# Layer norm statistics of the first three output tiles moved to ScalarE, and the selector matrices in a transfer of their own

## The chip, the core and the metric

One core of one Trainium2 chip runs the whole program. The metric is the time of one execution in device microseconds (us). The kernel before was timed three times: 891.20, 893.87 and 894.52 us, with the median at 893.87 us. One further execution was profiled. It took 891.03 us, and the profile covers 889.1 us of it (the span).

## What is computed

One inference step of a one-layer decoder, for 512 prompt tokens and 32 sample tokens, all in fp32. The front scales and shifts the input by vectors that come from a condition `c` (nine rows: one for the prompt, eight for the samples). Then follow one large input projection, a windowed attention (branch A) and a gated delta rule (branch B). The back merges the branches, multiplies by `w_out` and applies a layer norm to each token's row of 1024 numbers.

```python
def layer_front(x, c, w_cond, b_cond, w_in):
    shift, scale, gate = jnp.split(jax.nn.silu(c) @ w_cond + b_cond, 3, axis=-1)
    h = x * (1 + scale[:, None]) + shift[:, None]
    return gate, split_columns(h @ w_in)
...
    merged = jax.nn.sigmoid(ga) * (ya @ w_branch_a) + jax.nn.sigmoid(gb) * (yb @ w_branch_b)
    r = (ALPHA * x + gate[:, None] * (merged @ w_out)).astype(jnp.float32)
    mu = jnp.mean(r, axis=-1, keepdims=True)
    var = jnp.mean(jnp.square(r - mu), axis=-1, keepdims=True)
    return ((r - mu) * lax.rsqrt(var + LN_EPS)).astype(dtype) * ln_g + ln_b
```

## The kernel before

**Recording and scheduling.** The kernel does not issue instructions as it is read. `body` records every operation with its operands; `Recorder.schedule` (line 450 on) then sets one fixed order for each engine by a list scheduler with its own cost table, and `emit` issues them. All engines run their own list in order. For that reason nearly all instructions carry line 727. A change of one cost or one dependency anywhere can move instructions in other places too, as the scheduler breaks its ties anew.

**Split products.** Each large product is done as three passes of TensorE on a high and a low part of both factors (`hhi`, `hlo` are the input, `hi`, `lo` a tile of weights, `pp` the PSUM bank). A projection tile has 128 output features by 544 tokens, in two halves of 272 tokens; a half is 24 matmuls. The pool of `pp` has two banks, so a half can start once the half before the previous one has been copied out of its bank.

**The front** (lines 902 to 1030). SyncE (its queue is SPq in the profile) issues all loads in one queue: `cT`, the condition weights `wc` in 16 pieces of 512 KB, the bias `bT`, the constants `cst`, the transposed input `xT` and the first weights `W`. `cst` is one table of 330 columns: the identity `ident`, the selector matrices `selc` and `selg`, `low16` and `dmask`. `cond_block` multiplies `wc` by the condition, copies the rows to `Y`, and multiplies `Y` by `selc` to turn the scale of each feature into a column (`pg<-cst,Y`). `gate_rows` uses `selc` and `selg` together, 73 columns, much later.

**The back** (lines 2292 to 2399). `product_out` multiplies the merged rows by `w_out`, for n = 0 and 1 (512 output columns each) and tt = 0 to 3 (128 tokens each); tile 3 is done in pieces of 256 columns. The sum over one piece leaves PSUM in `scalar_tensor_tensor` into `r` (times the gate `gp`), then `tensor_add` adds the scaled input `xr`, then `bn_stats` takes the piece's statistics. All three run on VectorE (DVE). `norm_out` (line 2332) joins the statistics with `bn_aggr` into `mv`, ScalarE (ACT) takes the square root, and VectorE does the subtraction with the weight `lng` (1024 columns), a reciprocal, and two halves with `lnb`. Each half is then stored to `y_p`. `samples_out` does the same for the 32 sample rows between n = 0 and n = 1. Tile 3 of n = 1 has a rank that puts it ahead on VectorE.

**A place in the middle.** Near the end of the attention for the prompt, four ACT table switches, a reciprocal of 512 columns (`kq`), the copies out of `pp` into `spare` (an activation on ScalarE, then a product on VectorE that frees the bank), the copy `crow` and the product `vr` stand close together. The change does not edit that code, but the new order differs there.

Of the kernel before, what the change touches and what calls it, by code (L numbers as in the profile page):

```python
# [11 lines left out]
F32 = mybir.dt.float32  # L12
F32R = mybir.dt.float32r
AF = mybir.ActivationFunctionType
# [5 lines left out]
D = 1024  # L20
# [58 lines left out]
def shape_constants():  # L79

    p = np.arange(128)
    b4, i4, h8 = p // 32, p // 8 % 4, p % 8
    blk = {}
    blk["ident"] = np.eye(128)
    blk["selc"] = (p[:, None] % 32 == np.arange(9)[None, :])
    tok = np.arange(2 * NS)
    blk["selg"] = (p[:, None] % 32 == 1 + tok[None, :] % NS // 4)
    blk["triu"] = (p[:, None] <= p[None, :])
    same = p[:, None] // 4 == p[None, :] // 4
    blk["btri"] = same & (p[:, None] <= p[None, :])  # L90
    blk["bones"] = same
    blk["low16"] = np.where(p[:, None] % 32 >= 16, -1.0, 0.0)
    blk["strict4"] = same & (p[:, None] < p[None, :])
    blk["dmask"] = np.where(p[:, None] <= p[None, :], 0.0, -BIG)
    blk["dmask_s"] = np.where(same & (p[:, None] <= p[None, :]), 0.0, -BIG)
    blk["bmask"] = (p[:, None] % 32 // 4 == np.arange(8)[None, :])
    blk["quarter"] = np.where(p[:, None] % 32 == p[None, :] % 32, 0.25, 0.0)
    blk["hmask"] = (p[:, None] % 4 == np.arange(4)[None, :])
    sab = np.zeros((128, 4, 4))
    for h4 in range(4):  # L100
        for g in range(2):
            sab[4 * g + h4::16, h4, g] = 1.0
# [677 lines left out]
def body(ctx, tc, io):  # L780
    rec = Recorder()
    pe, ve, se, ge, sp = rec.engines()
    mv = sp
# [28 lines left out]
        return psp.tile([128, 512], F32, name="pp", tag="pp")  # L812


    cst = consts.tile([128, CONST[0].shape[1]], F32, name="cst")
    tables = {"early": cst}

    def take(gen, n):
        for _ in range(n):
# [3 lines left out]
    def C(name, where="early"):  # L823
        a, n = CCOLS[name]
        return tables[where][:, a:a + n]
# [38 lines left out]
    def to_features(pv, k, rows):  # L864

        for i in range(4):
            pe.matmul(pv[:, k + i, 0:9], rows[:, 128 * i:128 * i + 128], C("selc"), start=True, stop=True)

    f16 = lambda t: t[:, :128].rearrange("p (a b) -> p a b", b=16)

# [15 lines left out]
    n = CONST[1].shape[1]  # L886
# [8 lines left out]
    with ExitStack() as fctx:  # L895
# [35 lines left out]
        def cond_block(part, at, m, other):  # L931
# [18 lines left out]
            pv = ps[:, 256:256 + 16 * m].rearrange("p (a b) -> p a b", b=16)  # L950
            with rec.together():
                for i in range(m):
                    pe.matmul(pv[:, i, 0:9], Y[:, 128 * i:128 * i + 128], C("selc"), start=True, stop=True)
# [55 lines left out]
        with rec.together():  # L1009
            for t in range(4):  # L1010
                m = 128 if t < 3 else 16
                pe.matmul(pv[0:m, 16 * t:16 * t + 9], Y[:, 128 * t:128 * t + m], C("selc"), start=True, stop=True)
# [713 lines left out]

    def sample_decays(nd):

        tables["d"] = d0.tile([128, CONST[2].shape[1]], F32, name="cd")
# [393 lines left out]

    def gate_rows():

        sel = cst[:, CCOLS["selc"][0]:CCOLS["selc"][0] + 73]
        yield gates_over
        for n in range(2):
            w = slice(512 * n, 512 * n + 512)
# [184 lines left out]
    bn = [o1.tile([128, 4 if tt == 3 else 2, 6], F32, name=f"bn{tt}") for tt in range(5)]  # L2314
    parts = lambda k: ((mhi[k], 0), (mhi[k], 1), (mlo[k], 0))

    def product_out(tt, c0, c1):
# [26 lines left out]
    def samples_out():  # L2344
# [14 lines left out]
        ve.bn_stats(bn[4][:, 0, :], q)  # L2359
        mv = o2.tile([128, 4], F32, name="mv")  # L2360
        ve.bn_aggr(mv[:, 0:2], bn[4][:, 0, :])
# [13 lines left out]
    for n in range(2):  # L2375
        if n:
            samples_out()
        for tt in range(4):
            xr, q = load_x(tt, n), r[tt]
            step = 256 if tt == 3 else 512  # L2380
            for c in range(512 * n, 512 * n + 512, step):
                po = product_out(tt, c, c + step)
                w = slice(c, c + step)
                at_end = tt == 3 and c == 768
                rec.rank = -2 * (n and tt == 3)
                with rec.together() if at_end else nullcontext():
                    ve.scalar_tensor_tensor(q[:, w], po, 0.5, gp[:, w], op0=OP.mult, op1=OP.mult)
                    ve.tensor_add(q[:, w], q[:, w], xr[:, c - 512 * n:c - 512 * n + step])
                    ve.bn_stats(bn[tt][:, c // step, :], q[:, w])
                    if at_end:  # L2390
                        mv = o2.tile([128, 4], F32, name="mv")
                        ve.bn_aggr(mv[:, 0:2], bn[tt].rearrange("p a b -> p (a b)"))
                rec.rank = 0
            if n:
                rec.rank = -2 * (tt == 3)
# [35 lines left out]
def lay_out(x):  # L2431
# [7 lines left out]
    d = {  # L2439
        "bias_p": bias_p,  # L2440
        "bias_s": bias_s,
        "const": CONST[0],
        "const_g": CONST[1],
        "const_d": CONST[2],
        "const_s": CONST[3],
        "const_q": CONST[4],
        "x": rows,
        "xT": rows.T.reshape(KT, 128, NT).transpose(1, 0, 2),
        "cT": c.T.reshape(KT, 128, 9).transpose(1, 0, 2),
# [59 lines left out]
```

## Time and profile before

| | us |
|---|---|
| median of three runs | 893.87 |
| profiled execution | 891.03 |
| its span | 889.1 |
| TensorE (PE) busy | 868.8 (98%) |
| VectorE (DVE) busy | 646.1 (73%) |
| ScalarE (ACT) busy | 453.9 (51%) |

The four times, 891.03, 891.20, 893.87 and 894.52 us, fall into two pairs. The profile's times are counted from the start of the span. A row of the timeline has the start, the duration, the engine, the instruction with its output and inputs, and in brackets the idle time just before it with what ended it. A row of the waits has the total, the number and the longest wait. A row of the windows has the length of the stretch, the busy time with the number of instructions for PE, PEld, DVE, ACT and POOL, the granted clock, the busy share of the DMA engines and the GB/s moved. A row of the groups has the count, the total and the mean ns of one. The clock granted to TensorE was 0.996 over the run.

### The profile page before, as it was taken

How to read it: one execution, taken by the hardware profiler on the slowest of the kernel's cores; microseconds unless marked ns; L12 is line 12 of the kernel's file. 1: busy time of each engine (PE TensorE's matmuls, PEld its weight loads, DVE VectorE, ACT ScalarE, POOL GpSimd, SP SyncE). 2: the span in 40 equal slices, each digit the busy share in tenths (PEclk: the TensorE clock that was granted, in tenths of full speed). 3: DMA queues.
4: the chain of work that ended last, by engine and by line, in shares of the span. 5: the costliest groups of instructions: out<-in, count | busy, mean ns of one | idle time of the engine just before them, and what ended most of it. 6: DMA issues, size and time to landing. Idle time of an engine off the chain costs nothing.

```text
span 889.1 us, 20805 instructions
## 1 busy us (share of the span) xinstructions
PE 868.8 (98%) x8212; PEld 821.2 (92%) x8212; DVE 646.1 (73%) x1338; ACT 453.9 (51%) x1083; POOL 70.0 (8%) x173
## 2 busy tenths in 40 slices
PE   8999999999999999999999998999999999999995
PEld 7899999899999999999999897999999999999884
DVE  3675447653379997489988647556999699998558
ACT  3555378844478834579734566653442222334321
POOL 0120011100001200000200100011010000001000
PEclk9999999999999999999999999999999999999998
DMA  9965785776879788888888675659969899987963
GB/s 343 337 207 178 228 281 180 237 265 197 273 218 316 242 278 297 279 274 272 272 272 263 223 231 166 199 186 281 349 228 375 275 421 403 352 306 236 355 211 120
DMA packets 106910, 236.18 MB, mean 266 GB/s; under 512 B 30407, under 2 KB 62481, under 8 KB 104125
## 3 DMA queue, kind: packets, MB, share of 16 engines
q1 hardware_dynamic: 106812, 234.86, 77.7%
q8 instruction: 64, 1.05, 0.5%
q14 instruction: 34, 0.27, 0.1%
HBM read 218.53 MB, written 103.97 MB: 363 GB/s over the span
## 4 chain that ended last, share of the span: by engine, by line
PE 89%; ACT 3%; DMA 2%; DVE 2%; SPq 1%; issue 1%; DVEq 0%; ACTq 0%
PE pp L727 68%; PE pg L727 9%; PE pd L727 8%; PE pb L727 4%; DMA wc<-in_w_cb 2%; SPq L727 1%; ACT L727 1%; DVE r L727 1%; DMA S<-in_state_delta 1%; ACT sq L727 1%; ACT hi L727 0%; DVE lo L727 0%; DVE zt L727 0%; ACT ext L727 0%; ACT acc L727 0%
## 5 line engine op out<-in xcount | busy, mean ns | idle before, releaser
L727 PE MATMUL pp<-hhi,hi 128*128 128x272 f32 x1360 | 399.8, 294 | 2.5 <-DVE spare L727 1.5
L727 PE MATMUL pp<-hlo,hi 128*128 128x272 f32 x1360 | 400.2, 294 | 0.0
L727 PE MATMUL pp<-hhi,lo 128*128 128x272 f32 x1360 | 399.2, 294 | 0.0
L727 PEld LDWEIGHTS pp<-hhi,hi 128*128 128x128 f32 x1360 | 256.3, 188 | 5.8 <-issue 1.8
L727 PEld LDWEIGHTS pp<-hhi,lo 128*128 128x128 f32 x1360 | 256.1, 188 | 3.9 <-issue 2.7
L727 PEld LDWEIGHTS pp<-hlo,hi 128*128 128x128 f32 x1360 | 256.6, 189 | 2.5 <-issue 1.5
L727 ACT ACTIVATE hi<-wt 128x1024 fp32r<-128x1024 f32 (+1 forms) x101 | 103.7, 1026 | 162.0 <-PE pp L727 137.3
L727 DVE TENSOR_TENSOR lo<-wt,hi 128x1024 fp32r<-128x1024 f32 (+1 forms) x101 | 119.0, 1179 | 80.3 <-ACT hi L727 78.6
L727 DVE SCALAR_TENSOR_TENSOR acc<-ext,cw,acc 128x568 f32<-128x568 f32 x72 | 57.8, 803 | 1.1 <-ACT acc L727 0.4
L727 ACT ACT_TABLE_LOAD x36 | 46.2, 1283 | 2.5 <-DVE acc L727 0.9
L727 DVE TENSOR_TENSOR slab<-slab 128x512 f32<-128x512 f32 (+1 forms) x66 | 43.1, 670 | 4.5 <-DMA slab<-in_ks 3.2
L727 DVE TENSOR_REDUCE slab<-slab 128x8 f32<-128x512 f32 (+2 forms) x66 | 42.9, 662 | 2.9 <-ACT slab L727 2.6
L727 ACT ACTIVATE zt<-pp 128x272 f32<-128x272 f32 x48 | 18.7, 390 | 41.0 <-PE pp L727 39.5
L727 PE MATMUL pp<-ybl,hi 128*128 128x272 f32 x128 | 37.0, 289 | 0.0
L727 PE MATMUL pp<-ybh,lo 128*128 128x272 f32 x128 | 37.0, 289 | 0.0
L727 PE MATMUL pp<-ybh,hi 128*128 128x272 f32 x128 | 36.8, 288 | 0.0
L727 ACT ACTIVATE P<-P,st 128x256 f32<-128x256 f32 (+1 forms) x64 | 31.1, 489 | 9.5 <-DVE st L727 8.8
L727 DVE CUSTOM_DVE_ANT_0 P<-pg,bias 128x256 f32<-128x256 f32 (+1 forms) x64 | 23.5, 402 | 13.0 <-PE pg L727 12.7
L727 POOL COPY cx<-ext 128x3 f32<-128x3 f32 (+1 forms) x48 | 22.2, 489 | 113.8 <-ACT ext L727 109.3
L727 ACT ACTIVATE spare<-pp 128x272 f32<-128x272 f32 (+1 forms) x32 | 16.2, 505 | 22.5 <-PE pp L727 22.4
L727 PEld LDWEIGHTS pp<-ybh,hi 128*128 128x128 f32 x128 | 24.2, 189 | 0.2
L727 PEld LDWEIGHTS pp<-ybl,hi 128*128 128x128 f32 x128 | 24.1, 188 | 0.2
(415 smaller groups left out, 1565.3 us busy)
## 6 DMA issues: line engine op xcount, KB each, us to landing
out_kv_s<-in_cache SPq DMA_DIRECT2D x144, 512.0 KB
wt<-in_w_in SPq DMA_DIRECT2D x85, 512.0 KB
out_kv_s<-in_cache SPq DMA_DIRECT2D x24, 496.0 KB
wc<-in_w_cb SPq DMA_DIRECT2D x16, 512.0 KB
slab<-in_ks SPq DMA_DIRECT2D x32, 256.0 KB
slab<-in_vs SPq DMA_DIRECT2D x32, 256.0 KB
kv<-in_ks SPq DMA_DIRECT2D x16, 512.0 KB
kv<-in_vs SPq DMA_DIRECT2D x16, 512.0 KB
```

The lines of the kernel that those rows point to most:

```text
L727: getattr(real[x.engine], x.name)(*map(arg, x.args), **{k: arg(v) for k, v in x.kw.items()})
```

## The change

Two edits. In the back, the tiles 0 to 2 no longer use `bn_stats` and `bn_aggr`. After the last `tensor_add` of the row, ScalarE makes a pass over 1024 columns that sums them (the mean), a small one that negates the mean, a second pass that squares the difference to the mean and sums it, and the square root as before. Tile 3 and the samples keep `bn_stats`. In the front, `selc` and `selg` become a table of 73 columns of their own, `sel`, loaded where `cst` was loaded; `cst` keeps 257 columns and is loaded after the condition weights.

```diff
-    for names in (("ident", "selc", "selg", "low16", "dmask"), ("selab", "sel16", "triu", "btri", "bones"),
+    for names in (("selc", "selg"), ("ident", "low16", "dmask"), ("selab", "sel16", "triu", "btri", "bones"),
...
             load_cond(1, c, m)
             if not c:
                 sp.dma_start(bT, io["bT"])
-                sp.dma_start(cst, io["const"])
+                sp.dma_start(sel, io["const_f"])
...
         for c, m in two_by_two:
             load_cond(0, c, m)
+        sp.dma_start(cst, io["const"])
...
-            mv = o2.tile([128, 4], F32, name="mv")
-            ve.bn_aggr(mv[:, 0:2], bn[tt].rearrange("p a b -> p (a b)"))
-        se.activation(mv[:, 2:3], mv[:, 1:2], AF.Sqrt, bias=eps5)
+            mv, sq = o2.tile([128, 4], F32, name="mv"), o1.tile([128, D], F32, name="sq")
+            se.activation(sq, q, AF.Copy, scale=1.0 / D, accum_out=mv[:, 0:1])
+            se.activation(mv[:, 3:4], mv[:, 0:1], AF.Copy, scale=-1.0)
+            se.activation(sq, q, AF.Square, bias=mv[:, 3:4], accum_out=mv[:, 1:2])
+            se.activation(mv[:, 2:3], mv[:, 1:2], AF.Sqrt, bias=eps5, scale=1.0 / D)
+        else:
+            se.activation(mv[:, 2:3], mv[:, 1:2], AF.Sqrt, bias=eps5)
...
-                    ve.bn_stats(bn[tt][:, c // step, :], q[:, w])
+                    if tt == 3:
+                        ve.bn_stats(bn[:, c // step, :], q[:, w])
```

**SyncE at the start.** The rows below are the queue of loads, in the difference of the two orders (- before, + now).

```order
 L727 DMA wc<-in_w_cb 128x1024
 L727 DMA bT<-in_bT 128x24
-L727 DMA cst<-in_const 128x330
+L727 DMA sel<-in_const_f 128x73
 L727 DMA xT<-in_xT 128x544
...
 L727 DMA wc<-in_w_cb 128x1024 x6
-L727 DMA wt<-in_w_in 128x1024 x3
+L727 DMA cst<-in_const 128x257
+L727 DMA wt<-in_w_in 128x1024 x2
 L727 DMA wc<-in_w_cb 128x1024 x2
+L727 DMA wt<-in_w_in 128x1024
```

The fourth transfer is 37 KB where it was 169 KB; the other 132 KB follow six pieces of `wc` later, and one weight tile `wt` has moved behind the last pieces of `wc`.

**VectorE in the middle, before.** `pp_7342` and `pp_7501` are the banks of two successive half tiles.

```order
L727 SCALAR_TENSOR_TENSOR rn_7447<-rn_7447,rc_6033 128x4
L727 RECIPROCAL kq_6962<-kq_6962 128x512
L727 SCALAR_TENSOR_TENSOR spare_7511<-spare_7511,pp_7342 128x272
L727 RECIPROCAL rn_7447<-rn_7447 128x4
L727 TENSOR_TENSOR kq_6962<-us_848,kq_6962 128x256
L727 TENSOR_TENSOR orow_7544<-pd_7321,rn_7447 128x512
L727 SCALAR_TENSOR_TENSOR spare_7511<-spare_7511,pp_7501 128x272
L727 SCALAR_TENSOR_TENSOR kq_6962<-us_848,kq_6962 128x256
```

The same place on VectorE now; the two banks are `pp_7320` and `pp_7446`.

```order
L727 SCALAR_TENSOR_TENSOR spare_7456<-spare_7456,pp_7320 128x272
...
L727 RECIPROCAL kq_6956<-kq_6956 128x512
L727 SCALAR_TENSOR_TENSOR S_7570<-S_7471,etot_899,pd_7479 128x128
L727 SCALAR_TENSOR_TENSOR rn_7481<-rn_7481,rc_6040 128x4
L727 TENSOR_TENSOR vr_7576<-pb_7539,rc_7305 128x512
L727 TENSOR_TENSOR lo_7585<-wt_7131,hi_7566 128x1024
L727 SCALAR_TENSOR_TENSOR spare_7456<-spare_7456,pp_7446 128x272
L727 TENSOR_TENSOR kq_6956<-us_888,kq_6956 128x256
L727 SCALAR_TENSOR_TENSOR ya_1829<-ya_1829,spare_7456 128x512
L727 RECIPROCAL rn_7481<-rn_7481 128x4
L727 SCALAR_TENSOR_TENSOR kq_6956<-us_888,kq_6956 128x256
```

The first of the two copies has moved ahead of the long reciprocal; `vr` and `lo` have moved in between the reciprocal and the second copy. On ScalarE the neighbours are now these:

```order
L727 ACTIVATE kq_6956<-pb_7491,small_101 128x512
L727 ACTIVATE vn_7522<-pd_7479,rc_6040 128x128
L727 ACTIVATE NB_5306<-pg_7503 128x4x32
L727 ACTIVATE crow_7533<-pb_7526 81x128
L727 ACT_TABLE_LOAD
L727 ACTIVATE P_7524,st_5161<-P_7524,st_5161 128x256
L727 ACTIVATE sq1_7482,rn_7481<-pd_7357 128x128
L727 ACTIVATE hi_7566<-wt_7131 128x1024
L727 ACTIVATE spare_7456<-pp_7446 128x272
```

Before, `kq` was followed by three table loads with the two activations of `spare` between and behind them, then `hi`, then `crow`; now `crow` stands ahead of the first table load.

**The end, VectorE now.** `r0` to `r3` are the four tiles; the rows start at the copy of tile 2 out of PSUM.

```order
L727 SCALAR_TENSOR_TENSOR r2_11325<-pp_11516,gp_10798 128x512
L727 SCALAR_TENSOR_TENSOR r0_11258<-r0_11258,mv_11536,lnb_11260 128x512 x2
L727 SCALAR_TENSOR_TENSOR r1_11292<-r1_11292,mv_11557,lng_11255 128x1024
L727 SCALAR_TENSOR_TENSOR r3_11362<-pp_11560,gp_10798 128x256
L727 RECIPROCAL mv_11557<-mv_11557 128x1
L727 TENSOR_TENSOR r2_11325<-r2_11325,xr_11534 128x512
L727 TENSOR_TENSOR r3_11362<-r3_11362,xr_11542 128x256
L727 SCALAR_TENSOR_TENSOR r1_11292<-r1_11292,mv_11557,lnb_11260 128x512
L727 BN_STATS bn_11490<-r3_11362 128x6
L727 SCALAR_TENSOR_TENSOR r1_11292<-r1_11292,mv_11557,lnb_11260 128x512
```

Behind these come tile 3's last piece, one `BN_AGGR`, and the norms of tiles 2 and 3, with tile 2's halves last. Before, the halves of tile 0 and the `lng` step of tile 1 stood ahead of the copy of tile 2, and `BN_STATS` of tile 2 and a second `BN_AGGR` stood among the last rows. ScalarE at the end now has this order:

```order
L727 ACTIVATE sq_11537,mv_11536<-r0_11258 128x1024
L727 ACTIVATE mv_11536<-mv_11536 128x1
L727 ACTIVATE sq_11537,mv_11536<-r0_11258,mv_11536 128x1024
L727 ACTIVATE mv_11536<-mv_11536,eps5_11247 128x1
L727 ACTIVATE sq_11558,mv_11557<-r1_11292 128x1024
L727 ACTIVATE mv_11557<-mv_11557 128x1
L727 ACTIVATE sq_11558,mv_11557<-r1_11292,mv_11557 128x1024
L727 ACTIVATE xr_11534<-xr_11534 128x512
L727 ACTIVATE mv_11557<-mv_11557,eps5_11247 128x1
L727 ACTIVATE xr_11542<-xr_11542 128x512
```

Tile 2's four activations follow. Before, only the square roots and the scaling of `xr` stood here. TensorE's own list has the same matmuls in both programs, 8212 in the profile; at the end of the program they stand in the same order.

More of the change, by code (lines that the diff above doesn't have):

```diff
@@ L812, in pp @@
         return psp.tile([128, 512], F32, name="pp", tag="pp")
-    cst = consts.tile([128, CONST[0].shape[1]], F32, name="cst")
-    tables = {"early": cst}
+    sel = consts.tile([128, CONST[0].shape[1]], F32, name="sel")
+    cst = consts.tile([128, CONST[1].shape[1]], F32, name="cst")
+    tables = {"first": sel, "early": cst}
     def take(gen, n):
@@ L866, in to_features @@
         for i in range(4):
-            pe.matmul(pv[:, k + i, 0:9], rows[:, 128 * i:128 * i + 128], C("selc"), start=True, stop=True)
+            pe.matmul(pv[:, k + i, 0:9], rows[:, 128 * i:128 * i + 128], C("selc", "first"), start=True, stop=True)
     f16 = lambda t: t[:, :128].rearrange("p (a b) -> p a b", b=16)
@@ L885, in body @@
     early_ = op.tile([128, NT], F32, name="cg", tag="o")
-    n = CONST[1].shape[1]
+    n = CONST[2].shape[1]
     tables["g"] = early_[:, 0:n]
@@ L952, in cond_block @@
                 for i in range(m):
-                    pe.matmul(pv[:, i, 0:9], Y[:, 128 * i:128 * i + 128], C("selc"), start=True, stop=True)
+                    pe.matmul(pv[:, i, 0:9], Y[:, 128 * i:128 * i + 128], C("selc", "first"), start=True, stop=True)
                 turn_over(idle[2])
@@ L1011, in body @@
                 m = 128 if t < 3 else 16
-                pe.matmul(pv[0:m, 16 * t:16 * t + 9], Y[:, 128 * t:128 * t + m], C("selc"), start=True, stop=True)
+                pe.matmul(pv[0:m, 16 * t:16 * t + 9], Y[:, 128 * t:128 * t + m], C("selc", "first"), start=True, stop=True)
         ve.tensor_copy(shifts[:, 0:3], pv[:, 0:48].rearrange("p (a b) -> p a b", b=16)[:, :, 0:9])
@@ L1727, in sample_decays @@
     def sample_decays(nd):
-        tables["d"] = d0.tile([128, CONST[2].shape[1]], F32, name="cd")
+        tables["d"] = d0.tile([128, CONST[3].shape[1]], F32, name="cd")
         sp.dma_start(tables["d"], io["const_d"])
@@ L2124, in gate_rows @@
     def gate_rows():
-        sel = cst[:, CCOLS["selc"][0]:CCOLS["selc"][0] + 73]
         yield gates_over
@@ L2313, in body @@
     r = [o1.tile([128, D if tt < 4 else 256], F32, name=f"r{tt}") for tt in range(5)]
-    bn = [o1.tile([128, 4 if tt == 3 else 2, 6], F32, name=f"bn{tt}") for tt in range(5)]
+    bn, bns = o1.tile([128, 4, 6], F32, name="bn"), o1.tile([128, 6], F32, name="bns")
     parts = lambda k: ((mhi[k], 0), (mhi[k], 1), (mlo[k], 0))
@@ L2358, in samples_out @@
         ve.tensor_add(q, q, xr)
-        ve.bn_stats(bn[4][:, 0, :], q)
+        ve.bn_stats(bns, q)
         mv = o2.tile([128, 4], F32, name="mv")
-        ve.bn_aggr(mv[:, 0:2], bn[4][:, 0, :])
+        ve.bn_aggr(mv[:, 0:2], bns)
         pm = pd()
@@ L2388, in body @@
                     ve.tensor_add(q[:, w], q[:, w], xr[:, c - 512 * n:c - 512 * n + step])
-                    ve.bn_stats(bn[tt][:, c // step, :], q[:, w])
+                    if tt == 3:
+                        ve.bn_stats(bn[:, c // step, :], q[:, w])
                     if at_end:
                         mv = o2.tile([128, 4], F32, name="mv")
-                        ve.bn_aggr(mv[:, 0:2], bn[tt].rearrange("p a b -> p (a b)"))
+                        ve.bn_aggr(mv[:, 0:2], bn.rearrange("p a b -> p (a b)"))
                 rec.rank = 0
@@ L2441, in lay_out @@
         "bias_s": bias_s,
[L2442 to L2446, printed above, removed]
+        "const_f": CONST[0],
+        "const": CONST[1],
+        "const_g": CONST[2],
+        "const_d": CONST[3],
+        "const_s": CONST[4],
+        "const_q": CONST[5],
         "x": rows,
```

## The prediction

> **What bounds the kernel now.** I read the page's busy shares first, then what TensorE waited for, then the stretches that the two edits touch.
>
> ```profile
> PE 868.8 (98%) x8212; PEld 821.2 (92%) x8212; DVE 646.1 (73%) x1338; ACT 453.9 (51%) x1083; POOL 70.0 (8%) x173
> ```
>
> TensorE is busy for 868.8 of 889.1 us. The change takes no matmul away, so all that it can win lies in the remaining 20.3 us. The waits of TensorE, and three windows, say where those are.
>
> ```profile
> PE pb L727 <- DMA wc<-in_w_cb: 2.0, 2, 1.4
> PE pp L727 <- DVE spare L727: 1.5, 1, 1.5
> PE pp L727 <- DVE zt L727: 1.0, 2, 0.5
> PE pb L727 <- ACT crow L727: 0.8, 1, 0.8
> ```
>
> ```profile
> 16.00:19.00 3.00, 1.62 (x12) 1.33 (x12) 2.39 (x4) 1.31 (x3) 0.00 (x0) 1.00 1.02 408
> 500.00:550.00 50.00, 47.30 (x394) 44.44 (x394) 28.70 (x72) 35.47 (x96) 1.82 (x5) 1.00 0.61 198
> 861.00:878.00 17.00, 16.96 (x97) 14.64 (x95) 14.16 (x27) 4.28 (x8) 0.00 (x0) 1.00 0.35 121
> 878.00:889.10 11.10, 0.00 (x0) 0.00 (x0) 7.68 (x15) 0.48 (x2) 0.00 (x0) 0.70 0.32 119
> ```
>
> The reader is to see three places. At the start TensorE waits for the condition weights while the DMA engines are full (share 1.02, 408 GB/s). At 500 to 550 it loses 50.00 − 47.30 = 2.70 us. After 878 it has nothing left for 11.1 us, and VectorE works off a backlog. The two edits act on the first and the last place; the new order acts on the middle.
>
> **The start.** These are timeline rows.
>
> ```profile
> 0.74 0.39 SPq L727 DMA_DIRECT2D cT<-in_cT  x1
> 2.12 0.43 SPq L727 DMA_DIRECT2D cst<-in_const  x1
> 2.44 0.26 ACT L727 ACTIVATE th<-cT 128x72 f32<-128x72 f32 x1 [0.43 <-DMA cT<-in_cT]
> 6.79 0.39 PE L727 MATMUL pg<-cst,Y 128*128 128x9 f32 x2 [0.38 <-DVE Y L727]
> 19.02 1.07 PE L727 MATMUL pb<-wc,cs 128*32 128x256 f32 x16 [1.40 <-DMA wc<-in_w_cb]
> ```
>
> The first use of a selector, at 6.79, waited for `Y` and not for the table, so an earlier selector by itself wins nothing. What wins is that 257 columns × 4 bytes × 128 rows = 132 KB leave the queue ahead of the piece of `wc` that TensorE waits for at 19.02. At 408 GB/s that is 132 / 408 = 0.32 us; the number of transfers to issue ahead of it is the same. From 19.02 on TensorE has work queued, so nearly all of it is passed on. I take **−0.3 us**, between 0 (the small transfer occupies the engines as long as the large one did) and −0.35. Above nothing it does not go: the queue ahead only gets shorter. The 132 KB come back behind six pieces of `wc`, where their cover is long:
>
> ```profile
> L727 PE MATMUL pb<-cst,KQ x64: 270/272/330, 62.6 to 525.2; 128*128 128x128 f32 x64
> ```
>
> The first use of another column of `cst` is at 62.6 us. Without that cover the price would be the same 0.32 us. On the last pieces of `wc` the transfer costs nothing either, since a weight tile of 512 KB moves behind them in exchange.
>
> The rows of `sel` are short, 292 bytes. The nearest row is `cT`, with 288: issued from 0.74, used at 2.44, so landed within 1.7 us, and `sel` has from 2.12 to 6.79.
> [...]
>
> **The end.** First the timeline before, TensorE and then VectorE.
>
> ```profile
> 871.87 0.39 PE L727 MATMUL pp<-wo1h,mlo 128*128 128x512 f32 x1
> 877.68 0.29 PE L727 MATMUL pp<-wo1h,mlo 128*128 128x256 f32 x1
> ```
>
> ```profile
> 867.34 0.68 DVE L727 TENSOR_TENSOR r<-r,xr 128x512 f32<-128x512 f32 x1
> 871.36 1.41 DVE L727 SCALAR_TENSOR_TENSOR r<-r,mv,lnb 128x512 f32<-128x512 f32 x2
> 872.69 1.28 DVE L727 SCALAR_TENSOR_TENSOR r<-r,mv,lng 128x1024 f32<-128x1024 f32 x1
> 873.96 0.67 DVE L727 SCALAR_TENSOR_TENSOR r<-pp,gp 128x512 f32<-128x512 f32 x1
> 875.15 0.42 DVE L727 SCALAR_TENSOR_TENSOR r<-pp,gp 128x256 f32<-128x256 f32 x1 [0.52 <-PE pp L727]
> 878.20 0.69 DVE L727 BATCH_NORM_STATS2 bn<-r 128x6 f32<-128x512 f32 x1
> 880.17 0.33 DVE L727 BATCH_NORM_AGGREGATE mv<-bn 128x2 f32<-128x24 f32 x2
> 884.44 1.41 DVE L727 SCALAR_TENSOR_TENSOR r<-r,mv,lnb 128x512 f32<-128x512 f32 x2
> ```
>
> Tile 2's product leaves TensorE at 871.87 + 0.39, about 872.3, yet VectorE copies it only at 873.96, behind tile 0's halves and tile 1's `lng` step. From 872.3 on VectorE works without a pause but one of 0.52 us until 885.85 (884.44 + 1.41), long after TensorE's end at 877.97. So the end is VectorE's sum of work after 872.3, 13.55 us. In the new order there go out of this sum: the pause of 0.52 (tile 1's `lng` step now fills the time until tile 3's piece is done at 875.15), `BN_STATS` of tile 2 at 0.69 less an overlap of 0.08 with its neighbours, and half of the two `BN_AGGR` less overlap, 0.12. There comes in what of tile 0's two halves was done before 872.3: 872.3 − 871.36 = 0.94. The sum is −0.52 − 0.61 − 0.12 + 0.94 = **−0.3 us**. The other `BN_STATS` that go lie before 872.3, where VectorE waited for TensorE in any case, and are worth nothing.
>
> That holds while ScalarE is in time. A pass over 1024 columns with a sum is not in the trace; these groups bound it (the last columns are total us and mean ns).
>
> ```profile
> L727 ACT ACTIVATE bias<-bias 128x1024 f32<-128x1024 f32 x4 | 4.3, 1073 | 0.0
> L727 ACT ACTIVATION_READ_ACCUMULATOR sq<-pb 128x1 f32 x64 | 13.3, 208 | 0.0
> L727 ACT ACTIVATE x1h<-xT,sc 128x512 fp32r<-128x512 f32 x8 | 5.7, 714 | 2.6 <-DVE sc L727 2.6
> L727 ACT ACTIVATE xr<-xr 128x512 f32<-128x512 f32 x8 | 5.0, 631 | 12.9 <-DMA xr<-in_x 12.8
> L727 ACT ACTIVATE rn<-rn 128x4 f32<-128x4 f32 x8 | 1.6, 204 | 0.1
> ```
>
> The sum pass is 1.07 + 0.21 = 1.28; the negation 0.20; the square pass 1.28 + 0.08 for an operand from memory (714 − 631 ns) = 1.36; the root 0.20 + 0.08 = 0.28. That is 3.12 us a tile one after another, about 3.0 with the overlap that neighbours on ScalarE show. The bounds are 2.6 (the sums free) and 3.6 (0.1 us of waiting at each of five hand-overs). Tile 0's row is complete at 867.34 + 0.68 = 868.02 in both orders, so tiles 0 and 1 are through ScalarE at 874.0; VectorE wants tile 1 after 872.3 + 0.61 + 1.33 = 874.24. The margin is 0.2 us, and each us beyond it is a us at the end: behind tile 1's `lng` step wait tile 3's copy and all the rest of VectorE's queue. With 3.6 a tile the loss is 1.0 and this term +0.7; with 2.6 it stays −0.3. Tile 2's passes start at about 876.5 and have until 880.1, so 0.6 us in hand. No table load comes in: ScalarE's list holds 36 in both programs.
>
> **The middle.** The scheduler's new order moves instructions through most of the program.
>
> ```profile
> 60.00:500.00 440.00, 439.06 (x4381) 418.95 (x4381) 317.76 (x739) 272.10 (x699) 41.46 (x115) 1.00 0.78 254
> ```
>
> TensorE lost only 440.00 − 439.06 = 0.94 us between 60 and 500, so nothing large can be won there, and I take no change; the one cluster that can be won is at 535 to 547.
>
> ```profile
> 535.74 1.28 ACT L727 ACT_TABLE_LOAD   x1
> 537.74 1.28 ACT L727 ACT_TABLE_LOAD   x1
> 543.50 0.26 ACT L727 ACTIVATE crow<-pb 81x128 f32<-81x128 f32 x1
> ```
>
> ```profile
> 537.75 3.35 DVE L727 RECIPROCAL kq<-kq 128x512 f32<-128x512 f32 x1 [1.84 <-ACT kq L727]
> 541.02 0.38 DVE L727 SCALAR_TENSOR_TENSOR spare<-spare,pp 128x272 f32<-128x272 f32 x1
> ```
>
> ```profile
> 541.46 0.39 PE L727 MATMUL pp<-hhi,hi 128*128 128x272 f32 x1 [1.54 <-DVE spare L727]
> 543.82 0.66 PE L727 MATMUL pb<-cst,uv 128*128 128x128 f32 x4 [0.83 <-ACT crow L727]
> 545.87 0.33 PE L727 MATMUL pb<-cst,kq 128*128 128x128 f32 x1 [0.34 <-DVE vr L727]
> ```
>
> The copy of a half tile stood behind the reciprocal of 3.35 us, so TensorE waited 1.54 for its bank; then 0.83 for `crow`, which stood behind the table loads; then 0.34. That is all of the 2.70. In the new order this copy is ahead of the reciprocal and `crow` ahead of the table load, so both waits should go. But the next half's copy is now behind the reciprocal, `vr` and `lo`. From TensorE's start of the matmul that `kq` needs I count, by these durations, 8.4 us until that copy is done, and 9.0 until TensorE wants the bank. The `kq` products then come about 0.75 us too early. I take a wait of 1.0 in place of 2.7, **−1.7 us**; the bounds are −2.7 (no wait) and +1.4 (the copy late by the whole reciprocal, 3.35, and 0.75 for `kq`: 4.1 in place of 2.7).
>
> **Sum.** −0.3 − 0.3 − 1.7 = −2.3 us. On the profiled execution, 891.03, this gives 888.7; on the median, 893.87, it gives 891.6. The four times fall in two pairs 3 us apart, so I start from their mean, (891.03 + 891.20 + 893.87 + 894.52) / 4 = 892.66, and predict 890.4.
>
> **The rivals.** First, *the cluster's wait only moves*: the second copy is late by what the first was. Then the middle gives nothing, and the time is 892.66 − 0.6 = 892.1. For it speaks that the reciprocal and the table loads are still there; against it the 0.6 us in hand. Second, *the cluster gets worse*, the case on the slow side: `lo` now stands between the reciprocal and the second copy and needs `hi` from ScalarE, which stands behind a table load. It decides from the point at which that copy ends 0.6 us later than I count; from there each us costs TensorE one. At the upper bound it is +1.4 − 0.6 = +0.8, so 893.4. Against it: `hi` has 3 us of slack behind the reciprocal. Third, *the two edits give nothing*: short rows occupy the queue as long as before, and ScalarE is late by 0.3 us; then only the order counts, 892.66 − 1.7 = 891.0.
>
> **How the numbers follow.** Chances: forecast 0.50, moved wait 0.27, worse 0.13, edits without effect 0.10. The range reaches from the lower pair with every bound won (891.1 − 2.7 − 0.6, and 0.6 of the 1.0 that `zt` costs) = 887.2 to the upper pair with the worse cluster (894.5 + 0.8) = 895.3. Half a per cent, 4.5 us, is about what a measurement of this kernel can tell from no change. No case moves the time by that much alone; the forecast does so only if the two pairs of times fall unluckily, or more waits go in the middle than I counted. I give faster 0.14, same 0.81, slower 0.05.
>
> **What would show it.** TensorE's wait for `wc` near 19 should end 0.3 us earlier. Between 500 and 550 TensorE should be busy for some 49 of 50 us, with no wait on the first copy of `spare`. ScalarE's four steps should take 3.0 us a tile, VectorE should copy tile 2 at once when its product is done, and 13.2 us should pass from there to VectorE's end. It would be wrong if TensorE's idle time between 60 and 830 grew, if a row on VectorE showed a wait for `sq`, or if the selector matmul at 6.79 waited for a DMA.

## The result, and the profile after

| | before | after |
|---|---|---|
| median of 12 runs each on one chip, us | 892.44 (891.20 to 894.52) | 897.69 (895.02 to 902.44) |
| profiled execution, us | 891.03 | 896.39 |
| its span, us | 889.1 | 894.6 |
| granted clock | 0.996 | 0.991 |

The changed kernel is slower: the ratio is 1.0063, 95% interval 1.0046 to 1.0080. The prediction was 890.4 us, no change that a measurement could tell, within a range of 887.2 to 895.3 us.

Both edits do what they were said to do, and the cluster at 535 to 547 is won outright. The time goes elsewhere. The first view is TensorE's busy time by stretch, for which the prediction had, before the change, only 60 to 500 and 500 to 550, and nothing between 550 and 861. First the kernel before, then the changed one (length, busy time with the number of matmuls, granted clock, DMA share, GB/s).

```profile
500.00:570.00 70.00, 67.30 (x627) 1.00 0.60 196
570.00:600.00 30.00, 30.00 (x360) 1.00 0.54 177
600.00:660.00 60.00, 59.82 (x663) 1.00 0.82 284
790.00:833.00 43.00, 42.51 (x330) 1.00 0.77 266
```

```profile
60.00:500.00 440.00, 438.37 (x4341) 1.00 0.78 252
500.00:570.00 70.00, 70.00 (x684) 1.00 0.61 197
570.00:600.00 30.00, 27.69 (x343) 0.89 0.54 177
600.00:660.00 60.00, 57.18 (x640) 1.00 0.78 271
790.00:833.00 43.00, 41.25 (x336) 1.00 0.76 257
```

Length less busy time is what TensorE lost:

| stretch | before | after | more lost |
|---|---|---|---|
| 60 to 500 | 0.94 | 1.63 | +0.7 |
| 500 to 570 | 2.70 | 0.00 | −2.7 |
| 570 to 600 | 0.00 | 2.31 | +2.3, and a clock of 0.89 |
| 600 to 660 | 0.18 | 2.82 | +2.6 |
| 790 to 833 | 0.49 | 1.75 | +1.3 |

The clock of 0.89 over 30 us is an estimate of 3.3 us more (0.11 of 30 us). With it the sum is +7.5; the start gave 1.2 back (17.85 in place of 19.02 for the matmul that waited for `wc`), which leaves 6.3, where the span grew by 5.5 us. The difference of 0.8 is not accounted for; equal windows do not hold equal work.

The next view has four rows of the list of what TensorE waited for in the changed kernel: total, number, longest.

```profile
PE pg L727 <- issue: 3.1, 2, 2.3
PE pp L727 <- DVE zt L727: 2.3, 3, 1.2
PE pd L727 <- DVE ys L727: 1.0, 1, 1.0
PE pg L727 <- DVE o L727: 0.9, 1, 0.9
```

`spare`, `crow` and `vr`, the three waits of the cluster, are gone. The largest entry had no row in the kernel before, where "issue" ended one wait of 0.39 us at 495; and it names no releaser: "issue" is time in which TensorE waited for nothing that the profile shows. The timeline has the place.

```profile
573.35 1.35 PE L727 MATMUL pg<-cst,st 128*4 128x32 f32 x72
577.01 0.40 PE L727 MATMUL pg<-cst,st 128*4 128x128 f32 x8 [2.31 <-issue]
```

A group of 80 small matmuls stops after 72 of them for 2.31 us. Before, it ran through:

```profile
578.25 1.66 PE L727 MATMUL pg<-cst,st 128*4 128x32 f32 x80
```

What stood around it on SyncE's queue and on the DMA engines:

```profile
569.45 0.34 SPq L727 DMA_DIRECT2D wt<-in_w_in  x1
569.84 1.14 SPq L727 DMA_DIRECT2D out_kv_s<-in_cache  x2
```

```profile
569.50:574.50 5.00, 5.00 (x182) 4.51 (x181) 2.42 (x7) 2.55 (x8) 0.57 (x2) 1.00 0.86 308
574.50:578.70 4.20, 1.89 (x55) 1.48 (x42) 0.56 (x2) 1.17 (x4) 0.00 (x0) 1.00 0.06 16
578.70:585.52 6.82, 6.82 (x37) 6.20 (x36) 3.82 (x7) 2.48 (x5) 0.00 (x0) 0.50 0.01 2
```

A weight tile and two cache copies, 1.5 MB, filled the DMA engines (share 0.86) until 574.5. TensorE stood still from 574.70 to 577.01, and from 578.70 to 585.52 its clock was granted at 0.50. In that stretch a matmul of 272 tokens started every 0.227 us (582.06 to 584.33, ten steps), behind it, at 1.00, every 0.125 (587.00 to 587.62, five steps).

What the group may have lacked stands on the page of the profile under the DMA queues: besides the data there is a queue that carries instructions.

```profile
q8 instruction: 65, 1.06, 0.5%
```

65 packets of 16 KB (1.06 MB / 65) for some 16,400 matmuls and weight loads: about one for 250 of TensorE's instructions. In the trace one of these packets starts at 562.79, the next only at 574.64, when the 1.5 MB were through, and TensorE goes on at 577.01. So the first theory, T, was: **TensorE ran out of instructions, because the piece it fetched waited behind bulk transfers**; the idle time then cost it its clock; the waits at 640 to 650 and 800 to 833 come from the new order as well; and the two edits by themselves win a little.

### The profile page after: what moved, and what is told of

It reads as the page before. It is cut to its first block, busy times and chain, and to the rows that moved or that the text cites. A ratio compares the mean times of both kernels' runs of the same rounds, so it can differ in the third digit from the quotient of the medians.

```text
span 894.6 us, 20823 instructions
## 1 busy us (share of the span) xinstructions
PE 871.2 (97%) x8212; PEld 823.5 (92%) x8212; DVE 643.2 (72%) x1330; ACT 460.0 (51%) x1097; POOL 64.7 (7%) x173
## 3 DMA queue, kind: packets, MB, share of 16 engines
q8 instruction: 65, 1.06, 0.5%
## 4 chain that ended last, share of the span: by engine, by line
PE 91%; ACT 3%; DVE 3%; issue 1%; DMA 1%; SPq 0%; DVEq 0%; ACTq 0%
PE pp L727 68%; PE pg L727 10%; PE pd L727 9%; PE pb L727 4%; DMA wc<-in_w_cb 1%; DVE r L727 1%; ACT L727 1%; ACT hi L727 1%; ACT ext L727 0%; ACT sq L727 0%; DVE lo L727 0%; ACT acc L727 0%; ACT P L727 0%; DVE zt L727 0%; DVE acc L727 0%
## 5 line engine op out<-in xcount | busy, mean ns | idle before, releaser
L727 POOL COPY cx<-ext 128x3 f32<-128x3 f32 (+1 forms) x48 | 25.3, 556 | 113.4 <-ACT ext L727 111.3
L727 ACT ACTIVATE k<-pp 128x272 f32<-128x272 f32 (+1 forms) x24 | 13.1, 544 | 22.0 <-PE pp L727 22.0
```

The source lines that it names most:

```text
L727: getattr(real[x.engine], x.name)(*map(arg, x.args), **{k: arg(v) for k, v in x.kw.items()})
```

## Experiments: which edit, or the order

All times are medians; each ratio is against runs of the kernel before on the same chip, with its 95% interval. Those runs had medians of 891.04 us for the first four experiments, 891.92 for the next four and 891.67 for the last three.

**One edit alone.** The first (e1; each run is called by the start of its label) keeps only the front edit, with all lines of the statistics as before. The second (e2) keeps only the back edit, with all lines of the constants as before. Of each the main line, against the changed kernel:

```diff
-            se.activation(sq, q, AF.Copy, scale=1.0 / D, accum_out=mv[:, 0:1])
+            ve.bn_aggr(mv[:, 0:2], bn[tt].rearrange("p a b -> p (a b)"))
```

```diff
-                sp.dma_start(sel, io["const_f"])
+                sp.dma_start(cst, io["const"])
```

> Only the front edit (the selector matrices as a first transfer of their own); statistics as before. On every engine its order is that of the changed kernel up to the last output tiles. Theory T (both edits gain a little, the loss is the new order: in a burst of small matmuls near 575 TensorE runs out of instructions, because the 16 KB piece that it fetches waits behind the weight tile and two cache copies, then its clock is halved for 6.8 us): 898.3 us, the changed kernel's 897.7 plus the 0.6 that the tail no longer gains; a gap of about 2.3 us in the pg<-cst,st row near 575 and a half clock behind it. Rival A (the statistics on ScalarE are what costs, by waits at the end): 892 or less, no loss. Rival B (each edit costs about half): near 895.

> Only the back edit (mean and variance of three tiles on ScalarE); constants in one transfer as before. On every engine its order is that of the kernel before up to the last output tiles. Theory T: 891.8 us, 0.6 below the kernel before, TensorE without a gap over 1 us near 575 and the clock at full speed until the end. Rival A (the statistics cost): 897 or more. Rival B: near 895.

Measured: the front edit alone 897.14 us, ratio 1.0064 (1.0038 to 1.0089), the whole loss. T is borne out only in part by the first: its gap near 575 is 1.05 us and not 2.3, its clock stays at 1.00 there, and the half clock comes at 644.57, behind the waits of 640 to 650. The back edit alone 891.81 us, ratio 1.0001 (0.9986 to 1.0015), nothing. Rivals A and B fall. Since the back edit leaves the order ahead of the last tiles as it was and the front edit moves it everywhere, this points to the order or to the transfer itself. T's 0.6 us for the tail did not show in the median (891.81 against 891.04). Nor did the clock stay whole until the end: in its profile it was 0.50 from 544.51 to 547.92, behind the cluster's waits, with TensorE in the order of before.

**Both edits in the old order.** The recorded operations are the changed kernel's; only their order, and the engine of each copy that may go to either, come from a list in place of the scheduler.

```diff
         rec.schedule()
+        in_order(rec)
```

> Both edits, but every engine keeps the order of the kernel before up to the first operation on r0 (the selectors' transfer stands where the constants' one stood, the rest of the constants ahead of the first raw weight tile); from there the order of the changed kernel. Theory T: the wait for wc near 19 is gone (1.2 us) and the tail is 0.6 shorter, nothing is lost between, so 890.6 us (890 to 891.6), no half clock before the end. Rival C (the split transfer itself costs, wherever the order stands): 895 or more. Rival D (the front's gain is given back at the next wait for a transfer): 891.8.

Measured: 891.07 us, ratio 0.9998 (0.9982 to 1.0013). So the edits cost nothing that can be measured and rival C falls: **the loss is the order's.** But they win nothing that can be measured either, and T's 1.8 us of gain fall with it (D, which has the front's gain given back, cannot be told from no gain). TensorE's waits in this kernel, with both edits in place:

```profile
PE pb L727 <- DMA wc<-in_w_cb: 2.2, 2, 1.4
PE pp L727 <- DVE spare L727: 1.5, 1, 1.5
PE pb L727 <- ACT crow L727: 0.8, 1, 0.8
```

The wait for `wc` is there in spite of the smaller first transfer, and the cluster's waits are back with the old order. The wait for `wc` comes and goes from execution to execution: with the same order up to there, the matmul behind it started at 17.69 in e1 and at 19.34 in e8. It started at 19.02, 18.41 and 19.50 in the three profiles without the front edit, and between 17.69 and 19.36 in the ten with it, 18.4 on the mean against 19.0. The predicted 0.3 us may well be in there; one profile, and the 1.2 us of the changed kernel's, cannot tell.

## Experiments: the gap at 575

**The two cache copies moved.** Nothing waits for these copies, so they can go elsewhere in SyncE's list. In e4 they go behind the eight `wv` loads (record 6901 is the last), in e8 much further back.

```diff
+        two = [x for x in rec.order if x[0] == "op" and x[1].n in (547, 548)]
+        rec.order = [x for x in rec.order if x not in two]
+        at = next(i for i, x in enumerate(rec.order) if x[0] == "op" and x[1].n == 6901) + 1
+        rec.order[at:at] = two
```

```diff
+        order = rec.order
+        for n, behind in ((547, 563), (548, 564)):
+            x = next(x for x in order if x[0] == "op" and x[1].n == n)
+            order.remove(x)
+            order.insert(next(i for i, y in enumerate(order) if y[0] == "op" and y[1].n == behind) + 1, x)
```

> The changed kernel; of SyncE's issues only two 512 KB cache copies, which nothing waits for, are moved from behind the weight tile near 569.5 to behind the eight wv loads (some 20 us later). Theory T: the instruction piece comes 2 to 3 us earlier, the gap of 2.31 us in the pg<-cst,st row near 575 and the half clock behind it (together 5.7 us) are gone: 892.0 us, and the lead over the kernel before at 590 is 2 to 3 us. Rival E (the gap is made by the small matmuls or by a wait that the trace does not show; the copies have no part): 897.7, gap and half clock as they were. Rival F (the gap goes but the clock drops anyway, by the idle time of before it): 895.4.

> The changed kernel; the two cache copies near 570 moved further than before, one behind the copy near 648 and one behind that near 661, where no load that TensorE waits for follows at once. Theory T2: as with the copies some 20 us later, no gap at 575 and no half clock there, but without the waits for S and rbo near 622 and 630 (0.99 and 1.40 us): 891.8 us (890.5 to 893.5, by whether the waits of 640 to 650 fall into one clock window). Rival J (the copies, wherever they go, push something else back by as much): 895 to 896.5.

Measured: e4 896.00 us, ratio 1.0051 (1.0031 to 1.0071); e8 894.85 us, ratio 1.0031 (1.0014 to 1.0048). The mechanism was right and the sum was not. This is the group in e4:

```profile
574.16 0.44 PE L727 MATMUL pd<-Tc,NTs 32*32 32x32 f32 x16
574.53 1.57 PE L727 MATMUL pg<-cst,st 128*4 128x32 f32 x80
```

All 80 in 1.57 us, no gap, and the clock stays at 1.00 there. Rivals E and F fall, F although its 895.4 was the nearest number. But the copies, put elsewhere, pushed back what e4 lists as new waits,

```profile
PE pg L727 <- DMA rbo<-dO: 1.4, 1, 1.4
PE pb L727 <- DMA S<-in_state_delta: 1.0, 1, 1.0
```

and the clock was halved after all, 70 us later (below). In e8 the two waits are gone, as expected, and a gap of 0.50 us stays, with the weight tile still ahead of the instructions. I had counted nearly all of the loss at 575 and expected 891.8; by 894.85 about half of it is there. Rival J has the better number but not the mechanism, for e8's list of waits has none for a transfer behind 575.

**The gap by the lead of the instructions.** The start of the instruction packet against the start of the group of 80, from every kernel that tells something, is a better test than the copies. The lead is the time by which the packet starts ahead of the group:

| kernel | packet starts | group starts | lead | gap in the group |
|---|---|---|---|---|
| after | 574.64 | 573.35 | −1.3 | 2.31 |
| e6 | 579.13 | 578.15 | −1.0 | 1.82 |
| e11 | 578.72 | 578.09 | −0.6 | 1.98 |
| e1 | 574.23 | 574.15 | −0.1 | 1.05 |
| e5 | 575.81 | 576.54 | +0.7 | 0.68 |
| e8 | 574.98 | 575.91 | +0.9 | 0.50 |
| e4 | 573.29 | 574.53 | +1.2 | 0 |
| before | 576.97 | 578.25 | +1.3 | 0 |
| e9 | 572.70 | 574.40 | +1.7 | 0 |

In the six with a gap TensorE goes on 2.3 to 2.8 us after the packet's start. A lead of 1.2 us was enough; in the four kernels that are not in the table (e2, e3, e7, e10) it is 3.9 to 5.9 us, and there is no gap. In the same order of TensorE the lead was −1.3 and −0.1 with the copies in front (after, e1) and +1.2 and +0.9 without (e4, e8).

The leads alone do not show that TensorE lacked instructions; a count does. Count TensorE's records in the trace (matmuls, weight loads and its few semaphore and drain records) from the start. The thirteen profiles have 19 stops of over 0.1 us that "issue" ended. Every one of them stands behind record 7105, 9665 or 11457, whatever matmul comes next, and these are 256 × 27 + 193, 256 × 37 + 193 and 256 × 44 + 193. At the end of each stop exactly 27, 37 or 44 of the packets of 16 KB had started, the last of them 2.25 to 2.79 us before. So by this count the packets hold 256 records each (the changed kernel has 16,593 records and 65 packets, 255 each), and every one of these stops lies where one piece of 256 ends and the next had not come.

The count also says what the order did. When a packet is asked for is not in the trace. But in no profile does a packet n behind the first start before TensorE has begun 256 × (n − 1) + 158 records, which is 291 records ahead of the place where TensorE would stop without it. Counted from there, packet 44 took 4.4 and 3.2 us with the copies in front (after, e1) and 1.9 and 2.2 us without (e4, e8), in the same order of TensorE, VectorE and ScalarE: the copies held it up. From the same place to the start of the group of 80 it is 3.1 us in the changed kernel's order and 7.0 us in the order of before. In the kernel before the packet took 5.7 us and did no harm. In e9, which has the copies in front too, it took 5.8 us, and the group starts 7.5 us behind the place.

## Experiments: the order in pieces

**The new order up to 560, the old one behind it, and the reverse.** Same edit as for e3, with other lists. The place where a list goes from one order to the other is called its seam.

> Both edits; every engine follows the changed kernel's order up to the last load of Tc (near 560 us), then the order of the kernel before for what is left, then, from r0 on, the changed kernel's. Theory T2 (the edits by themselves move nothing that can be measured; the new order gains 3.1 to 3.9 us between 475 and 575 and loses more behind it: 2 to 4.7 at 575 to 600, 2.6 to 4 at 600 to 650, 1.5 at 800 to 833): the gain is kept and the losses are gone, 891.0 - 3.2 = 887.8 us (886.8 to 889). Rival G (the gain of the cluster is not kept: in the old order behind it the same loads and copies end last, so its waits come back later): 890.5 to 891.5.

> Both edits; the order of the kernel before up to the last load of Tc (near 560 us), the changed kernel's order for the rest. Theory T2: the losses without the gain, 891.0 + 7.5 = 898.5 us (896.5 to 900; the lower end if the piece of instructions comes in time here, since its phase is another). Rival H (the loss is made ahead of 560, by what the new order of the front leaves late, and only shows behind it): 891 to 892.

Measured: e6 899.07 us, ratio 1.0096 (1.0065 to 1.0127), within 0.6 us of what was expected. The losses lie behind 560 and come without any help from the front; rival H falls. The other half missed: e5 891.14 us, ratio 0.9991 (0.9978 to 1.0005), where I had expected 887.8. The gain was partly kept: at the seam TensorE waits for the transfer `Tc`, which is issued where the new order has it, at 561.75, and wanted by the old order 4.7 us later (9.3 us lie between in the changed kernel, 10.5 in the kernel before). And the group of 80 stops there too.

```profile
566.46 0.44 PE L727 MATMUL pd<-Tc,NTs 32*32 32x16 f32 x32 [0.91 <-DMA Tc<-dtz]
578.20 0.87 PE L727 MATMUL pg<-cst,st 128*4 128x32 f32 x36 [0.68 <-issue]
```

Between 60 and 500 it lost 2.58 us, 1.6 more than the kernel before: the new order has small matmuls near 368 that stop with "issue" in the same way (0.83 to 1.86 us in the profiles that keep it).

**The new order where it wins only.** The first of these has a seam at 345 more than the second; the third takes the second's order without either edit.

> Both edits; the changed kernel's order up to about 345 us, the order of before up to about 440, the changed kernel's up to the last load of Tc, the order of before up to r0, the changed kernel's to the end: the new order where it gained, the old one where the new lost (1.4 to 1.9 us between 350 and 375, and all behind 560). Theory T2: 1 to 1.6 us below the kernel that keeps the new order up to 560, about 886.5 us (885.5 to 888). Rival G: 890 or more. Rival I (the gain of the cluster needs the order of 350 to 440 as well): 888 to 890.

> Both edits; the order of the kernel before up to about 440 us, the changed kernel's up to the last load of Tc (near 560), the order of before up to r0, the changed kernel's to the end: the run with the cluster alone, without the change of order near 345 whose seam made a wait of 1.86 us. Theory T2 (the edits by themselves move nothing that can be measured; the new order is worth about 3 us between 475 and 575): 1.2 us that run was below the kernel before, and 2 more without the seam: 891.5 - 3.2 = 888.3 us (887 to 889.5), TensorE without a wait of over 1 us between 60 and 830. Rival G (the gain is given back behind the cluster): 890.5 or more.

> Neither edit: the kernel before, its own constants and statistics, with nothing but the order of the run beside it (before up to about 440, the changed kernel's up to the last load of Tc, before to the end). Theory T2: all of the gain is the order's, 0.3 to 0.6 above the run beside it: 888.7 us (887.5 to 890). Rival K (the gain needs the split transfer or the statistics): 891 or more.

Measured: e7 890.74 us, ratio 0.9992 (0.9976 to 1.0009), a miss of 4 us. The seam had made a wait of its own, which is less than half of the miss:

```profile
347.71 0.39 PE L727 MATMUL pp<-hhi,lo 128*128 128x272 f32 x1 [1.86 <-DVE lo L727]
```

Why the rest is missing is not known; the profiled execution, 888.16 us, was the shortest of its twelve. Without that seam, e9: 887.93 us, ratio 0.9950 (0.9930 to 0.9970), faster than both kernels and within 0.4 us of what was expected; rival I falls. Its stretches from 500 to 660 have the new order's gain and none of its losses:

```profile
500.00:570.00 70.00, 69.35 (x692) 1.00 0.62 204
570.00:600.00 30.00, 30.00 (x343) 1.00 0.63 206
600.00:660.00 60.00, 60.00 (x666) 1.00 0.86 293
```

And e10, **neither edit, the order alone**: 888.38 us, ratio 0.9956 (0.9940 to 0.9972). All of the gain that can be measured is the order's; rivals G and K fall. The two edits together are worth 0.45 us at the median, less than the half width of either interval (1.8 and 1.4 us). The seam near 560 is not free: `Tc` makes TensorE wait there for 0.65 us in e9's profile and for 1.98 us in e10's, which was the longest of its seven executions (889.31 us).

**The old order from 600 on, the gap left in.**

> Both edits; the changed kernel's order up to about 600 us, so with the gap at 575, then the order of before up to r0, then the changed kernel's. Theory T2: the waits for zt and ys of 640 to 650, the half clock that sometimes follows them, and the waits of 800 to 833 (together 4 to 5 us) are gone, the gap near 575 stays: 896.9 - 4.5 = 892.4 us (891 to 893.5). Rival L (those waits come of what is late ahead of 600, not of the order behind it): 896 or more.

Measured: 893.09 us, ratio 1.0023 (1.0005 to 1.0041); rival L falls. The waits of 640 to 650 belong to the order there: they are gone in e11 and in e5, which have the old order at that place, and present in e6, which has the new. But e11's seam has waits of its own. In its profile, one of four executions out of twelve near 897 us (896.46), they are the only ones between 600 and 660:

```profile
PE pb L727 <- DMA S<-in_state_delta: 1.7, 2, 1.5
PE pd L727 <- DMA S<-in_state_delta: 0.9, 1, 0.9
```

In the changed kernel the waits of 640 to 650 are these, TensorE first, then VectorE:

```profile
640.74 0.39 PE L727 MATMUL pp<-hhi,hi 128*128 128x272 f32 x1 [0.56 <-DVE zt L727]
646.44 0.49 PE L727 MATMUL pd<-ys,nd 128*128 128x128 f32 x2 [0.98 <-DVE ys L727]
648.09 0.40 PE L727 MATMUL pp<-hhi,hi 128*128 128x272 f32 x1 [1.16 <-DVE zt L727]
```

```profile
643.76 1.22 DVE L727 TENSOR_TENSOR S<-S,us 128x1024 f32<-128x1024 f32 x1
644.90 1.29 DVE L727 TENSOR_TENSOR ybl<-zt,ybh 128x512 fp32r<-128x512 f32 x2
646.10 0.28 DVE L727 TENSOR_TENSOR ys<-rr,pd 128x128 f32<-128x128 f32 x1
646.46 1.23 DVE L727 TENSOR_TENSOR lo<-wt,hi 128x1024 fp32r<-128x1024 f32 x1
647.60 0.78 DVE L727 SCALAR_TENSOR_TENSOR zt<-zt,pp 128x272 f32<-128x272 f32 x2
```

VectorE works without a pause, and the short copies that TensorE waits for (`zt` frees a bank, `ys` feeds a matmul) stand behind products of 1.2 us that TensorE does not wait for at that time. In the kernel before, the copy `zt` of 646.01 stood ahead of `lo`. It is the same pattern as in the cluster at 541, at another place.

## Why the prediction was wrong

- **The base, 892.66.** Right by luck: the four times looked like two pairs, but the twelve runs of the kernel before show no pairs, and their median of 892.44 us happens to lie near the mean of the four.
- **The start, −0.3.** Not refuted and not shown: 18.4 against 19.0 us on the mean of ten and three profiles, with a spread of 1.7, and nothing in the medians (e3: 891.07 against 891.04). The selector matmul waited for `Y` and not for a transfer, as said; the short rows of `sel` cost nothing visible.
- **The end, −0.3.** ScalarE's four steps, which the trace of before could not show, are now there:

```profile
873.81 1.06 ACT L727 ACTIVATE sq<-r 128x1024 f32<-128x1024 f32 x1 [2.21 <-DVE r L727]
874.78 0.18 ACT L727 ACTIVATION_READ_ACCUMULATOR sq<-r 128x1 f32 x1
874.99 0.20 ACT L727 ACTIVATE mv<-mv 128x1 f32<-128x1 f32 x1
875.23 1.15 ACT L727 ACTIVATE sq<-r,mv 128x1024 f32<-128x1024 f32 x1
876.50 0.30 ACT L727 ACTIVATE mv<-mv,eps 128x1 f32<-128x1 f32 x1
```

  From 873.81 to 876.80 it is 2.99 us, against 3.0 predicted. VectorE's wait for `sq`, named as a sign of error, is there and harms nothing, because VectorE was ahead of TensorE at that time:

```profile
876.51 1.28 DVE L727 SCALAR_TENSOR_TENSOR r<-r,mv,lng 128x1024 f32<-128x1024 f32 x1 [2.13 <-ACT sq L727]
878.05 0.69 DVE L727 SCALAR_TENSOR_TENSOR r<-pp,gp 128x512 f32<-128x512 f32 x1 [0.19 <-PE pp L727]
888.24 2.74 DVE L727 SCALAR_TENSOR_TENSOR r<-r,mv,lnb 128x512 f32<-128x512 f32 x4
```

  From the copy of tile 2 to VectorE's end (888.24 + 2.74 = 890.98) it is 12.93 us, before 13.55 from the end of tile 2's product, predicted 13.2. Counted from TensorE's last matmul, VectorE ended 7.9 us later in the three profiles without this edit (before, e1, e10), 7.5 in nine with it and 7.3 in e2: 0.4 us or more earlier, about as forecast. The step from there to the end of the span, which the sum left out, took 3.2 to 3.6 us without the edit and 3.5 to 3.8 with it, so how much of the 0.4 reaches the end cannot be told, and the medians show none. The third rival, no effect of the two edits, is as near to the medians as the forecast.
- **The cluster, −1.7.** Right in its kind and too small: all 2.70 us went, the bound that I had given, since the second copy came in time and made no wait of its own. The moved wait and the worse cluster, rivals one and two, did not come about.
- **"I take no change", for 60 to 500, and no word on 550 to 833.** This is the step that failed. The text said that the new order "moves instructions through most of the program" and then priced it at the one place where the old order had waits. A new order takes away old waits only where there are some, and can make new ones anywhere: +0.7, +2.3 with 3.3 for the clock, +2.6 and +1.3 us. The sign named for it, TensorE's idle time between 60 and 830, is exactly what grew. The worst case that the range allowed for the order was +0.8 us, at the cluster; a cost of new waits anywhere else was put at nothing, and it came to 10.2 us in this profile. Against the kernel before on the same chip, the new order is worth −3.3 us at its best place (e10: 888.38 against 891.67) and +7.2 us behind 560 (e6: 899.07 against 891.92). With the stop near 368 (0.83 to 1.86 us) that is an estimate of +4.7 to +5.8, and the changed kernel's median lies 5.25 us above that of the kernel before.

## What to carry to other kernels

Where a scheduler breaks its ties anew, price an edit in two parts: what it does in the old order (here nothing that the medians show) and what the new order does; the second has no bound from the old profile, since every stretch that had no idle time can only lose. Ask of the new order on each engine not only whether old waits go, but also which short copies that TensorE needs now stand behind long products, and which bulk transfers now stand just ahead of a burst of small matmuls. Then the useful part can be kept and the rest put back, which was worth 0.4% here without either edit.

## What the runs showed of the hardware

**Instructions come by DMA, and a burst of small matmuls can outrun them.** Queue q8 of the page (65 packets, 1.06 MB), the count and the table of leads above are the evidence: all 19 stops with "issue" lie at 256 n + 193 of TensorE's records, with n packets of 16 KB begun. Where packet 44 started 1.2 us or more ahead of the 80 small matmuls they ran through; where it started 1.3 us behind their start the gap was 2.31 us.

**The clock switched on a grid of 3.41 us.** In every profile the clock's switches lie whole multiples of 3.413 us apart (changed kernel: 578.70, 585.52 and 885.90, that is 2 and 88 steps, with (885.90 − 578.70) / 90 = 3.413). A window is here one step of this grid. In five profiles with the same order there (after, e1, e4, e6, e8), the same two waits came with or without a half clock, and it went with where the windows' bounds fell. The changed kernel's waits of 0.98 and 1.16 us lay in two windows, and the clock stayed at 1.00:

```profile
643.55:646.96 3.41, 2.40 (x18) 1.00 0.90 359
646.96:650.38 3.42, 2.17 (x16) 1.00 0.59 198
```

In e4 both lay in one, and the next window ran at half the clock (so too in e1 and e8, with 0.97 over 600 to 660; in e6 they lay in two, and the clock stayed at 1.00 over 600 to 660):

```profile
644.23:647.64 3.41, 1.31 (x8) 1.00 0.74 267
647.64:651.06 3.42, 3.42 (x17) 0.50 1.16 395
```

Up to TensorE's last matmul, five profiles have a window with 1.7 to 2.1 us of idle time (1.72, 1.83, 1.72, 2.10, 2.14 in after, e1, e2, e4, e8) that was followed by a window or two at 0.50; windows with up to 1.6 us never were (the longest of these was 1.33 us in the kernel before and 1.24 in the changed one). One with 1.88, in e10, was not, so idle time alone does not tell which were; what does is not shown. I take the place of the bounds to be a part of the spread of the changed kernel, whose runs lie between 895.02 and 902.44 us. The clock granted over each run agrees: it is 0.989 in the two longest (900.90 and 902.44 us) and 0.992 or 0.993 in seven of the eight shortest, and 0.004 of 895 us is, by estimate, 3.6 us. That windows with two waits are behind it is not shown, since only one execution of each kernel has a profile; and e11's profile, with 896.46 us far above its median of 893.09, has no half clock ahead of TensorE's end but the waits for `S`.
